# Seven block products for two thirds of the feed-forward pairs of a two-layer trunk

## The chip, the cores and the metric

The kernel runs on one core of a Trainium2 chip. The metric is the device time of one execution in microseconds, the median of several runs; lower is better. TensorE multiplies, VectorE and ScalarE do elementwise work, GpSimd a few sums, and SyncE issues most transfers. The trace records every instruction of one profiled execution.

## What is computed

The reference is a trunk of two layers on 512 tokens of width 1024, all in float32. Layer 0 mixes with a causal convolution module, layer 1 with differential attention. Each layer then has a SwiGLU feed-forward of width 2816 and a gated per-layer input. The change touches the feed-forward alone:

```python
def swiglu(x, w_gate, w_up, w_down):
    return (jax.nn.silu(x @ w_gate) * (x @ w_up)) @ w_down
...
for i in range(DEPTH):
    h = h + (conformer_conv(rms_norm(h, ...)) if i % 2 == 0 else diff_attention(rms_norm(h, ...)))
    u = rms_norm(h, ffn_norm_g[i])
    h = h + swiglu(u, ffn_w_gate[i], ffn_w_up[i], ffn_w_down[i])
    gate = jax.nn.sigmoid(rms_norm(h, ple_norm_g[i]) @ ple_w_gate[i])
    h = h + gate * (p[i] @ ple_w_proj[i])
```

## The kernel before

**Layout.** Activations lie transposed: features on the 128 partitions, the 512 tokens along the row. The residual is eight tiles `h[0..7]` of 128 x 512. A weight tile of 128 x 1024 holds one chunk of 128 output features, as eight blocks of 128 x 128, one for each chunk of the input features.

**Precision.** A float32 product is made of three float32r products. Each operand is split into a high part (a ScalarE copy to float32r) and a low part (the rest, by a VectorE subtraction). `mm3` (L153 to L157) multiplies low by high, high by low and high by high into one PSUM tile. `weight()` (L137 to L151) loads the next tile into `wraw` (two buffers, SyncE's queue), copies it into `whi` on ScalarE (L148) and subtracts into `wlo` on VectorE (L150); `whi` and `wlo` have four buffers each.

**Norms.** `Norm.chunk` (L179) scales a residual chunk by its gain, splits it into the tiles A0 to A15, and sums the squares. The factor 1/rms of each token, `rb`, comes later (`diagonal`, `rows`), so the feed-forward multiplies its products by `rb` afterwards (L582, L584).

**The feed-forward** (`ffn`, L566 to L596) goes through the 22 chunks of hidden features in three parts of 8, 8 and 6 (`PARTS`). For each chunk it loads a gate and an up tile, makes 24 matmuls of 512 columns for each into PSUM tiles `pg` and `pu`, multiplies by `rb`, applies Silu on ScalarE (L583), multiplies (L585) and splits the result into a hidden tile B (L587, L588). After a part, `linear` (L538) multiplies the part's hidden tiles by the down weights, one output chunk after another, the first two together, and `add` (L592) adds to the residual; in the last part each finished residual chunk goes on to the next norm.

**Names used below.** A chunk is one hidden chunk, a pair is two neighbouring ones. PSUM has the tags `mm` (four buffers), `sc` (two) and `tp` (two). In SBUF `wk` has four, `big` five buffers. `pp` is the projection of the per-layer input, made before and held in C and D tiles. The attention's `stage_s` (L755) puts the scores of a head's two halves into the two halves of one `sc` tile when they are at most 256 wide, and reads each on VectorE (L775 to L778). The last chunk of the last `ple` (L598) is made as two runs of 24 matmuls of 256 columns (`CUTS`).

**What sets the order.** The kernel is written in one order; a planner then fixes the order of each engine's own queue at build time, from its estimate of when each instruction is ready, and sets the waits and the reuse of buffers. On the chip each queue is worked in that fixed order.

Of the kernel before, what the change touches and what calls it, by code (L numbers as in the profile page):

```python
# [12 lines left out]
F32 = mybir.dt.float32  # L13
F32R = mybir.dt.float32r
AF = mybir.ActivationFunctionType
ALU = mybir.AluOpType
# [4 lines left out]
P = 128  # L21
S = 512
D = 1024
NC = D // P
# [52 lines left out]
PACK = True  # L77
E1 = True
GLO = 1
QKV = (("q", 0, (0, 0, 0, 0)), ("v", 0, (0, 1, 1, 0)), ("q", 1, (1, 1, 2, 2)), ("q", 2, (0, 1, 2, 0)), ("v", 1, (1, 2, 2, 2)), ("q", 3, (0, 2, 0, 1)))  # L80


@with_exitstack
def trunk(ctx, tc, xT, pT, wts, diag, dww, vec, rel, onehot, lamv, out):
    nc = tc.nc
    V, A, G, T = nc.vector, nc.scalar, nc.gpsimd, nc.tensor
# [19 lines left out]
    big = lambda dt=F32, shape=(P, S): sb(list(shape), "big", 5, dt)  # L106
    f = lambda ap: ap.bitcast(F32)
# [6 lines left out]
    def col(name, i=0):  # L114
        a, _ = VEC[name]
        return vt[:, a + i : a + i + 1]
# [7 lines left out]
    t = wk()[:, 0:P]  # L124
# [4 lines left out]
    t = tp()  # L129
# [4 lines left out]
    wnext = [0]  # L134
    loaded = [None]

    def weight(n=1024, pieces=1, between=(), eng=V, after=None):  # L137
        i = wnext[0]
        wnext[0] += 1
        raw = sb([P, 1024], "wraw", 2)  # L140
        hi = sb([P, 1024], "whi", 4, F32R)
        lo = sb([P, 1024], "wlo", 4, F32R)
        for k in range(pieces):
            cut = slice(k * n // pieces, (k + 1) * n // pieces)
            loaded[0] = nc.sync.dma_start(raw[:, cut], wts[i, :, cut])
            if k < len(between):
                between[k]()
            A.copy(hi[:, cut], raw[:, cut])  # L148
            with tc.issue_after(after.ins) if after else nullcontext():
                eng.tensor_tensor(lo[:, cut], raw[:, cut], f(hi[:, cut]), ALU.subtract)  # L150
        return hi, lo  # L151

    def mm3(acc, a, b, first, last):  # L153
        (ah, al), (bh, bl) = a, b
        T.matmul(acc, al, bh, start=first, stop=False)  # L155
        T.matmul(acc, ah, bl, start=False, stop=False)  # L156
        return T.matmul(acc, ah, bh, start=False, stop=last)  # L157
# [75 lines left out]
    norm = Norm("conv_g")  # L233
# [36 lines left out]
    y = []  # L270
# [160 lines left out]
    for c in range(NC):  # L431
        wa, wg = pairs[c]
        if c == 0:
            pg = half(wg)
            norm.diagonal()
            pa = half(wa)
            rb = norm.rows()
# [3 lines left out]
        if c > 0:  # L441
            pg = half(wg)
# [5 lines left out]
        tg, ta = big(), big()  # L448
# [59 lines left out]
    r = rsqrt_cols(vs[:, 0:4], 4, 1.0)  # L508
# [17 lines left out]
    z = []  # L526
# [36 lines left out]
    linear(NC, z, add_conv, 3, first=(None, last_add[0], scaled[1]))  # L563


    def ffn(norm, after):  # L566
        rb = None
        for at, (f0, n) in enumerate(PARTS):
            hid = []
            for i in range(n):  # L570
                wg, wu = weight(), weight()
                pg, pu = mm(), mm()
                for k in range(NC):
                    mm3(pg, wpart(wg, k), norm.u[k], k == 0, k == NC - 1)
                if rb is None:
                    norm.diagonal()
                for k in range(NC):
                    mm3(pu, wpart(wu, k), norm.u[k], k == 0, k == NC - 1)
                if rb is None:
                    rb = norm.rows()  # L580
                tg, tu = big(), big()
                V.tensor_tensor(tg, pg, rb, ALU.mult)  # L582
                A.activation(tg, tg, AF.Silu)  # L583
                V.tensor_tensor(tu, pu, rb, ALU.mult)  # L584
                V.tensor_tensor(tu, tu, tg, ALU.mult)  # L585
                hl = sb([P, 2, S], f"B{i}", 1, F32R)
                A.copy(hl[:, 0], tu)  # L587
                V.tensor_tensor(hl[:, 1], tu, f(hl[:, 0]), ALU.subtract)  # L588
                hid.append((hl[:, 0], hl[:, 1]))

            def add(m, acc):
                V.tensor_tensor(h[m], acc, h[m], ALU.add)  # L592
                if at == len(PARTS) - 1:
                    after.chunk(m)

            linear(n, hid, add, 2)  # L596
# [27 lines left out]
                gate(*part)  # L624

    n2 = Norm("ple_g0")
    ffn(norm, n2)
    norm = Norm("attn_g")
    ple(n2, pp, lambda m, cut: norm.chunk(m))

# [9 lines left out]
    for k in range(2):  # L640
        t = tp()
# [263 lines left out]
    norm = Norm("ffn_g1")  # L905
# [4 lines left out]

    linear(NC, ot, add_attn, 2, heads_until, step)
    n2 = Norm("ple_g1")
    ffn(norm, n2)

    def store(m, cut):
        nc.sync.dma_start(out[m][:, cut], h[m][:, cut])
# [30 lines left out]
def _layout(a):  # L947
# [25 lines left out]
    qkv = a["attn_w_qkv"][0]  # L973
    for what, at, _ in QKV:
        if what == "v":
# [70 lines left out]
```

## Time and profile before

| | us |
|---|---|
| median of 3 runs | 1307.87 (1307.86 to 1312.03) |
| the profiled execution: its span | 1308.0 |
| feed-forward of layer 0, part one: first products to first down sum | about 224 to 321 |
| part two: products, then down | 355 to 443, then to 487 |
| part three: products, then down | 487 to 553, then to 586 |
| feed-forward of layer 1, parts two and three | about 1030 to 1118 and 1162 to 1228 |

No separate device time is kept for the profiled execution; its span lies 0.1 us from the median. Times on the trace's rows count from the span's start. A row of the timeline has the start, the duration, the engine, the line, the operation, "out<-in" by the program's names with the shape, and in brackets the idle time before it with what ended it. A row of a grouped view has the count, the busy time, the mean duration in ns, and the idle time before the group's instructions. Two instructions of one engine can overlap by a little, so the distance between starts is what a full queue pays.

### The profile page before, as it was taken

To read this page: it belongs to the slowest core of one execution; us is meant where nothing else is said; L and a number is where in the kernel's file an instruction comes from. 1 tells how busy PE (TensorE), PEld (TensorE's weight loads), DVE (VectorE), ACT (ScalarE), POOL (GpSimd) and SP (SyncE) were. 2 spreads that over 40 slices of the span, in tenths; PEclk is the share of its full clock that TensorE was granted. 3 is DMA by queue.
4 is the path that set the end of the run, shared out by engine and by line. 5 is a ranking of instruction groups with operands and counts; after the bars stand their busy time and mean duration, and the time that the engine had idled before them with its cause. 6 is when DMAs were issued, how large, how long until landed. Compare 5 with 4: busy or idle time off the path is not lost. (4 is left out here: it accounts for less than half of the span.)

```text
span 1308.0 us, 15405 instructions
## 1 busy us (share of the span) xinstructions
PE 1278.6 (98%) x5904; PEld 1055.7 (81%) x5904; DVE 741.2 (57%) x1142; ACT 522.1 (40%) x827; POOL 248.2 (19%) x207
## 2 busy tenths in 40 slices
PE   8999999999999999999999998999999999999998
PEld 5888678888888888888888886878888888888887
DVE  6898646444344434456678888845543344334445
ACT  5642445332122212254566667734332233223332
POOL 4754323000000000032335535122000000000030
PEclk8999889999999999999999998999999999999999
DMA  6654313322323232232222211213323223222231
GB/s 219 229 166 156 106 33 129 96 98 87 106 96 97 88 104 94 80 122 83 80 91 92 89 58 59 87 48 114 97 97 97 97 97 97 97 97 89 83 119 65
DMA packets 46838, 131.97 MB, mean 101 GB/s; under 512 B 5379, under 2 KB 9987, under 8 KB 46764
## 3 DMA queue, kind: packets, MB, share of 16 engines
q1 hardware_dynamic: 44640, 127.55, 29.6%
q10 hardware_dynamic: 2124, 3.43, 0.8%
q8 instruction: 46, 0.75, 0.2%
q14 instruction: 28, 0.23, 0.1%
HBM read 126.75 MB, written 4.21 MB: 100 GB/s over the span
## 5 line engine op out<-in xcount | busy, mean ns | idle before, releaser
L148 ACT CAST whi<-wraw 128x1024 fp32r<-128x1024 f32 (+2 forms) x214 | 218.6, 1026 | 566.3 <-PE mm L157 349.5
L155 PE MATMUL mm<-A,wlo 128*128 128x512 f32 (+1 forms) x1096 | 423.9, 391 | 4.8 <-ACT A L169 2.7
L156 PE MATMUL mm<-A,whi 128*128 128x512 f32 (+1 forms) x1096 | 428.0, 392 | 0.4
L157 PE MATMUL mm<-A,whi 128*128 128x512 f32 (+1 forms) x1096 | 425.3, 389 | 0.0
L150 DVE TENSOR_TENSOR wlo<-wraw,whi 128x1024 fp32r<-128x1024 f32 (+2 forms) x210 | 260.5, 1244 | 70.9 <-ACT whi L148 70.6
L155 PEld LDWEIGHTS mm<-A,wlo 128*128 128x128 f32 x1096 | 206.2, 188 | 49.6 <-DVE wlo L150 3.7
L156 PEld LDWEIGHTS mm<-A,whi 128*128 128x128 f32 x1096 | 206.6, 188 | 46.4 <-DVE A L170 3.0
L157 PEld LDWEIGHTS mm<-A,whi 128*128 128x128 f32 x1096 | 206.6, 188 | 43.1 <-issue 1.0
L189 POOL TENSOR_TENSOR acc<-acc,wk 128x512 f32<-128x512 f32 x42 | 67.4, 1604 | 787.7 <-issue 660.2
L156 PE MATMUL mm<-B,whi 128*128 128x512 f32 x352 | 137.5, 391 | 0.0
L157 PE MATMUL mm<-B,whi 128*128 128x512 f32 x352 | 137.5, 391 | 0.0
L155 PE MATMUL mm<-B,wlo 128*128 128x512 f32 x352 | 137.2, 392 | 0.0
L592 DVE TENSOR_TENSOR h<-mm,h 128x512 f32<-128x512 f32 x48 | 33.0, 691 | 122.7 <-PE mm L157 122.7
L584 DVE TENSOR_TENSOR big<-mm,rb 128x512 f32<-128x512 f32 x44 | 30.4, 691 | 126.2 <-PE mm L157 126.2
L582 DVE TENSOR_TENSOR big<-mm,rb 128x512 f32<-128x512 f32 x44 | 30.4, 691 | 99.4 <-PE mm L157 93.0
L157 PEld LDWEIGHTS mm<-B,whi 128*128 128x128 f32 x352 | 66.1, 188 | 14.6
L155 PEld LDWEIGHTS mm<-B,wlo 128*128 128x128 f32 x352 | 66.1, 188 | 14.2
L156 PEld LDWEIGHTS mm<-B,whi 128*128 128x128 f32 x352 | 66.0, 188 | 14.2
L157 PE MATMUL mm<-whi,A 128*128 128x512 f32 x192 | 75.6, 395 | 0.0
L156 PE MATMUL mm<-wlo,A 128*128 128x512 f32 x192 | 75.0, 396 | 0.0
L155 PE MATMUL mm<-whi,A 128*128 128x512 f32 x192 | 74.8, 397 | 0.0
L214 POOL TENSOR_TENSOR r<-v,mhalf 128x8 f32<-128x8 f32 (+1 forms) x31 | 47.4, 1529 | 122.8 <-DVE v L212 100.4
(198 smaller groups left out, 1402.0 us busy)
## 6 DMA issues: line engine op xcount, KB each, us to landing
wraw<-in_wts SPq DMA_DIRECT2D x194, 512.0 KB, 3.5
wraw<-in_wts SPq DMA_DIRECT2D x16, 384.0 KB, 2.9
D<-in_diag SPq DMA_DIRECT2D x22, 256.0 KB, 4.9
C<-in_diag SPq DMA_DIRECT2D x16, 256.0 KB, 4.7
h<-in_xT SPq DMA_DIRECT2D x8, 256.0 KB, 5.6
bias<-scr ACTq DMA_DIRECT2D x8, 256.0 KB, 3.3
out_t<-h SPq DMA_DIRECT2D x7, 256.0 KB, 2.0
wraw<-in_wts SPq DMA_DIRECT2D x4, 256.0 KB, 5.2
```

The lines of the kernel that those rows point to most:

```text
L148: A.copy(hi[:, cut], raw[:, cut])
L150: eng.tensor_tensor(lo[:, cut], raw[:, cut], f(hi[:, cut]), ALU.subtract)
L155: T.matmul(acc, al, bh, start=first, stop=False)
L156: T.matmul(acc, ah, bl, start=False, stop=False)
L157: return T.matmul(acc, ah, bh, start=False, stop=last)
L189: self.last = self.eng.tensor_tensor(self.acc, self.acc, sq, ALU.add)
L214: last_pow[0] = G.tensor_tensor(r[:, :n], v[:, :n], mhalf[:, :n], ALU.pow)
L582: V.tensor_tensor(tg, pg, rb, ALU.mult)
L584: V.tensor_tensor(tu, pu, rb, ALU.mult)
L592: V.tensor_tensor(h[m], acc, h[m], ALU.add)
```

## The change

The first two pairs of a feed-forward stay as they are. While they run, a generator, stepped a few times in each chunk (`STEPS`), makes normed operands: `us[c]` = residual times gain times `rb`, split into `un[c]` in C and D tiles. From the third pair on the products use `un`, so nothing is multiplied by `rb` afterwards and Silu reads PSUM.

During the third and fourth pair the generator makes the combinations of the activations for seven block products: the operand is cut into four blocks, two halves of the input chunks (0 to 3 and 4 to 7) by two halves of the tokens (256 each). Four of the seven operands are differences of blocks, made by VectorE and split into the A tiles, which the raw operands have left by then; three are blocks themselves.

All pairs of parts two and three (four and three of them) then go through `strassen`, once for the two gate tiles and once for the two up tiles; one such run is called a group. `operands` makes the weight side: q gets the first halves of both weight tiles by a plain load, and an adding transfer on GpSimd's queue adds the second tile's two halves to them, so that two of the four weight sums come by transfer; the other two (s2, s4) are made by VectorE. Seven products of 4 blocks, 12 matmuls of 256 columns each, fill four PSUM tiles in the order 1, 5, 7, 2, 6, 4, 3, and VectorE combines them with seven sums (five instructions). A group takes four buffers each of `whi` and `wlo`.

```diff
-    def ffn(norm, after):
+    def ffn(norm, after, space):
...
+        def normed():
+            us = []
+            for c in range(NC):
...
+                V.scalar_tensor_tensor(t, h[c], col(norm.g, c), rb, ALU.mult, ALU.mult)
...
+                A.copy(hi, t)
+                V.tensor_tensor(lo, t, f(hi), ALU.subtract)
+                un.append((hi, lo))
+                yield
...
+            for c in (0, 2):
+                n3, t2 = (wk(F32, (P, 2, H2)) for _ in range(2))
+                for name in (5, 7, 6, 4):
...
+                    for j in range(2):
...
+                        V.tensor_tensor(t[:, j], x, y, ALU.subtract)
+                    i = 2 * (4 * (c // 2) + (5, 7, 6, 4).index(name))
+                    hi, lo = (sb([P, 2, H2], f"A{i + j}", 1, F32R) for j in range(2))
+                    A.copy(hi, t)
+                    V.tensor_tensor(lo, t, f(hi), ALU.subtract)
...
+        def operands(i):
+            turn[0] += 1
+            q = sb([P, 2, S], qtags[turn[0] % 3], 2)
+            nc.sync.dma_start(q, bass.AP(wts.tensor, wts.offset + i * P * 1024, [[1024, P], [2 * P * 1024, 2], [1, S]]))
+            nc.gpsimd.dma_start(q, wts[i + 2].rearrange("p (a s) -> p a s", a=2), accum_op=ALU.add)
+            r = sb([P, 2, S], "wraw", 2)
+            nc.sync.dma_start(r, wts[i].rearrange("p (a s) -> p a s", a=2))
+            z = sb([P, S], "bias", 2)
+            nc.sync.dma_start(z, wts[i + 2, :, S:])
...
+            p = ring()
+            split(flat(r), *p)
+            w[1], w[2] = half(p, first), half(p, low)
+            p = ring()
+            split(flat(q), *p)
+            w[7], w[5] = half(p, first), half(p, low)
+            s2, s4 = sb([P, S], "wth", 2), sb([P, S], "wtl", 2)
+            V.tensor_tensor(s2, q[:, 1], r[:, 0], ALU.add)
+            V.tensor_tensor(s4, s2, r[:, 1], ALU.add)
+            p = ring()
+            w[6], w[3] = half(p, first), half(p, low)
+            split(s2, *w[6])
+            split(s4, *w[3])
+            p = ring()
+            w[4] = half(p, first)
+            split(z, *w[4])
+            return w
+
+        def strassen(i):
+            w = operands(i)
+            def product(acc, name):
+                for k in range(4):
+                    mm3(acc, wpart(w[name], k), comb[name][k], k == 0, k == 3)
+            one, two, three, four = sc(), mm(), mm(), tp()
+            t, e, g = wk(), big(), big()
+            first, second = slice(0, H2), slice(H2, S)
+            product(one[:, first], 1)
+            A.copy(t[:, first], one[:, first])
+            A.mul(t[:, second], one[:, first], -1.0)
+            product(three[:, first], 5)
+            product(three[:, second], 7)
+            product(two[:, first], 2)
+            product(two[:, second], 6)
+            V.tensor_tensor(e, two, t, ALU.add)
+            V.tensor_tensor(
+                g.rearrange("p (a s) -> p a s", a=2), three.rearrange("p (a s) -> p a s", a=2),
+                e[:, second].unsqueeze(1).to_broadcast([P, 2, H2]), ALU.add,
+            )
+            V.tensor_tensor(e[:, second], three[:, second], g[:, first], ALU.add)
+            product(four[:, second], 4)
+            V.tensor_tensor(g[:, second], four[:, second], g[:, second], ALU.add)
+            product(four[:, first], 3)
+            V.tensor_tensor(g[:, first], four[:, first], g[:, first], ALU.subtract)
+            return e, g
...
+                if (at, pair) in SEVEN:
...
+                    gs = strassen(i)
+                    for t in gs:
+                        A.activation(t, t, AF.Silu)
+                    us = strassen(i + 1)
+                    for o, (t, g) in enumerate(zip(us, gs)):
+                        V.tensor_tensor(t, t, g, ALU.mult)
...
+                        A.copy(hs, t.rearrange("p (a s) -> p a s", a=2))
+                        V.tensor_tensor(ls, t.rearrange("p (a s) -> p a s", a=2), f(hs), ALU.subtract)
+                    continue
+                x = norm.u if seen < RAW_PAIRS else un
```

`RAW_PAIRS` is 2, `STEPS` is (0, 2, 3, 3) and two in every later chunk, `SEVEN` lists the pairs of parts two and three, and `SPACE` names the C and D tiles that each layer's feed-forward may use: with one of six buffers held by `pp`, three turn as q.

More of the change, by code (lines that the diff above doesn't have):

```diff
@@ L563, in trunk, with feed, ring, split @@
     linear(NC, z, add_conv, 3, first=(None, last_add[0], scaled[1]))
-    def ffn(norm, after):
+    def ffn(norm, after, space):
+        qtags, utags = space
         rb = None
+        un = []
+        comb = {}
+        uses = [None]
+        def normed():
+            us = []
+            for c in range(NC):
+                if c < 6:
+                    if c % 2 == 0:
+                        two = sb([P, 2, S], qtags[c // 2], 2)
+                    t = two[:, c % 2]
+                else:
+                    t = sb([P, S], "wth", 2)
+                us.append(t)
+                V.scalar_tensor_tensor(t, h[c], col(norm.g, c), rb, ALU.mult, ALU.mult)
+                tags = utags[c]
+                if len(tags) == 1:
+                    hi, lo = both(sb([P, 2, S], tags[0], 2, F32R))
+                else:
+                    hi, lo = (sb([P, S], t_, 1, F32R) for t_ in tags)
+                A.copy(hi, t)
+                V.tensor_tensor(lo, t, f(hi), ALU.subtract)
+                un.append((hi, lo))
+                yield
+            uses[0] = un
+            comb[1] = [tuple(t[:, :H2] for t in un[k]) for k in range(4)]
+            comb[2] = [tuple(t[:, :H2] for t in un[4 + k]) for k in range(4)]
+            comb[3] = [tuple(t[:, H2:] for t in un[4 + k]) for k in range(4)]
+            while uses[0] is not None:
+                yield
+            for k in (5, 7, 6, 4):
+                comb[k] = []
+            for c in (0, 2):
+                n3, t2 = (wk(F32, (P, 2, H2)) for _ in range(2))
+                for name in (5, 7, 6, 4):
+                    t = t2 if name == 6 else n3 if name == 7 else wk(F32, (P, 2, H2))
+                    for j in range(2):
+                        top, low = us[c + j], us[4 + c + j]
+                        b11, b12, b21, b22 = top[:, :H2], top[:, H2:], low[:, :H2], low[:, H2:]
+                        x, y = {5: (b12, b11), 7: (b12, b22), 6: (b11, n3[:, j]), 4: (b21, t2[:, j])}[name]
+                        V.tensor_tensor(t[:, j], x, y, ALU.subtract)
[3 more added lines that the diff above has]
+                    V.tensor_tensor(lo, t, f(hi), ALU.subtract)
+                    comb[name] += [(hi[:, j], lo[:, j]) for j in range(2)]
+                    yield
+        making = [normed()]
+        def feed(n=1):
+            for _ in range(n):
+                if making:
+                    try:
+                        next(making[0])
+                    except StopIteration:
+                        making.pop()
+        turn = [0]
+        def ring():
+            return [sb([P, 1024], t, 4, F32R) for t in ("whi", "wlo")]
+        def split(raw, hi, lo):
+            A.copy(hi, raw)
+            V.tensor_tensor(lo, raw, f(hi), ALU.subtract)
+        def operands(i):
[7 more added lines that the diff above has]
+            nc.sync.dma_start(z, wts[i + 2, :, S:])
+            first, low = slice(0, S), slice(S, 2 * S)
+            flat = lambda t: t.rearrange("p a s -> p (a s)")
+            half = lambda w, c: tuple(t[:, c] for t in w)
+            w = {}
+            p = ring()
[34 more added lines that the diff above has]
+                e[:, second].unsqueeze(1).to_broadcast([P, 2, H2]), ALU.add,
+            )
+            V.tensor_tensor(e[:, second], three[:, second], g[:, first], ALU.add)
[4 more added lines that the diff above has]
+            return e, g
+        seen = 0
@@ L568, in ffn @@
         for at, (f0, n) in enumerate(PARTS):
             hid = []
[L570 to L589, printed above, removed]
+            for pair in range(n // 2):
+                hi, lo = (sb([P, 2, S], f"B{2 * pair + k}", 1, F32R) for k in range(2))
+                for k in range(2):
+                    hid.append((hi[:, k], lo[:, k]))
+                if (at, pair) in SEVEN:
+                    i = wnext[0]
+                    wnext[0] += 4
+                    gs = strassen(i)
[4 more added lines that the diff above has]
+                        V.tensor_tensor(t, t, g, ALU.mult)
+                        first, step = (H2, H2) if o else (0, S + H2)
+                        hs, ls = (bass.AP(x.tensor, x.offset + first, [list(x.ap[0]), [step, 2], [1, H2]]) for x in (hi, lo))
+                        A.copy(hs, t.rearrange("p (a s) -> p a s", a=2))
+                        V.tensor_tensor(ls, t.rearrange("p (a s) -> p a s", a=2), f(hs), ALU.subtract)
+                    continue
+                x = norm.u if seen < RAW_PAIRS else un
+                for i in range(2):
+                    wg, wu = weight(), weight()
+                    pg, pu = mm(), mm()
+                    for k in range(NC):
+                        mm3(pg, wpart(wg, k), x[k], k == 0, k == NC - 1)
+                    if rb is None:
+                        norm.diagonal()
+                    for k in range(NC):
+                        mm3(pu, wpart(wu, k), x[k], k == 0, k == NC - 1)
+                    if rb is None:
+                        rb = norm.rows()
+                    tg, tu = big(), big()
+                    if x is un:
+                        A.activation(tg, pg, AF.Silu)
+                        V.tensor_tensor(tu, pu, tg, ALU.mult)
+                    else:
+                        V.tensor_tensor(tg, pg, rb, ALU.mult)
+                        A.activation(tg, tg, AF.Silu)
+                        V.tensor_tensor(tu, pu, rb, ALU.mult)
+                        V.tensor_tensor(tu, tu, tg, ALU.mult)
+                    A.copy(hi[:, i], tu)
+                    V.tensor_tensor(lo[:, i], tu, f(hi[:, i]), ALU.subtract)
+                    feed(STEPS[2 * seen + i] if 2 * seen + i < len(STEPS) else 2)
+                seen += 1
+                if seen == RAW_PAIRS:
+                    assert len(un) == NC, len(un)
+                    feed()
+                    uses[0] = None
@@ L626, in trunk @@
     n2 = Norm("ple_g0")
-    ffn(norm, n2)
+    ffn(norm, n2, SPACE[0])
     norm = Norm("attn_g")
@@ L912, in trunk @@
     n2 = Norm("ple_g1")
-    ffn(norm, n2)
+    ffn(norm, n2, SPACE[1])
     def store(m, cut):
```

7 lines of the change are left out of this document (added).

## The prediction

> **What bounds the kernel now.** First the page's totals:
>
> ```profile
> span 1308.0 us, 15405 instructions
> PE 1278.6 (98%) x5904; PEld 1055.7 (81%) x5904; DVE 741.2 (57%) x1142; ACT 522.1 (40%) x827; POOL 248.2 (19%) x207
> ```
>
> TensorE is busy nearly all the time; VectorE has 43% to spare on average. An average hides stages, so next the busy times by stage: the first feed-forward's part one (224 to 312), two (355 to 443) and three (487 to 553), and, for later use, four stages in which VectorE is loaded harder.
>
> ```profile
> 33.00:65.00 32.00, 31.69 (x176) 26.97 (x175) 28.84 (x34) 19.17 (x28) 22.79 (x17) 1.00 0.66 226
> 65.00:98.00 33.00, 31.17 (x174) 26.86 (x173) 29.68 (x36) 16.07 (x23) 16.85 (x14) 1.00 0.51 167
> 224.00:312.00 88.00, 88.00 (x392) 72.65 (x391) 42.87 (x53) 26.95 (x34) 3.20 (x2) 1.00 0.29 96
> 355.00:443.00 88.00, 88.00 (x389) 72.84 (x389) 39.93 (x48) 26.07 (x32) 0.00 (x0) 1.00 0.29 96
> 487.00:553.00 66.00, 66.00 (x293) 54.64 (x292) 29.20 (x36) 18.63 (x24) 0.00 (x0) 1.00 0.28 86
> 700.00:760.00 60.00, 58.39 (x303) 49.27 (x302) 52.58 (x130) 42.54 (x96) 34.94 (x35) 1.00 0.24 79
> 760.00:820.00 60.00, 53.27 (x278) 45.11 (x277) 49.72 (x141) 41.72 (x99) 25.30 (x26) 0.91 0.23 74
> ```
>
> The columns are stage, length, busy PE, PEld, DVE, ACT, POOL with counts, granted clock, DMA share, GB/s. In the feed-forwards PE is busy without a gap, at clock 1.00, with VectorE at 40 to 49%. The list of waits for parts two and three says the same:
>
> ```profile
> DVE big L584 <- PE mm L157: 44.3, 14, 3.6
> ```
>
> VectorE waits for matmuls there, 14 times for 3.2 us. The stage is matmul time, so fewer matmul columns shorten it, as long as VectorE and the queues keep up.
>
> **TensorE's part.** In part two the same VectorE instruction, released by the same matmul, comes seven chunks apart at:
>
> ```profile
> 360.01 0.69 DVE L582 TENSOR_TENSOR big<-mm,rb 128x512 f32<-128x512 f32 x1 [3.15 <-PE mm L157]
> ...
> 436.17 0.69 DVE L582 TENSOR_TENSOR big<-mm,rb 128x512 f32<-128x512 f32 x1 [2.21 <-PE mm L157]
> ```
>
> 76.16/7 = 10.88 us a chunk of 48 matmuls, 226.7 ns for each of 512 columns; a pair of chunks is 96 matmuls, 21.76 us. The change turns a pair into 2 groups (gate, up) x 7 products x 4 blocks x 3 = 168 matmuls of 256 columns. That width stands at the end of the kernel, 48 in a row:
>
> ```profile
> 1297.69 0.28 PE L155 MATMUL mm<-A,wlo 128*128 128x256 f32 x1
> ...
> 1303.32 0.28 PE L157 MATMUL mm<-A,whi 128*128 128x256 f32 x1
> ```
>
> 5.63/47 = 119.8 ns, more than half of 226.7: about 13 ns a matmul do not shrink. So a pair costs 168 x 0.1198 = 20.13 us and saves 1.63, not an eighth of 21.76 (2.72). Seven pairs in each of two feed-forwards: 14 x 1.63 = 22.9 us off, 1285.1 if nothing else waits. The Trainium skill (TensorE: Matmul & The Clock Gate, Back-to-back issue gap) gives N/2.4 + 2.5 ns for a warm isolated matmul, 215.8 and 109.2 ns; by it the gain would be 33.2 us and the time 1274.8 (estimate). This trace has 11 ns more on each matmul, which counts double at half the width, so the rows decide.
>
> **VectorE's part.** Its prices, back to back and in a dependent chain:
>
> ```profile
> 529.17 0.69 DVE L584 TENSOR_TENSOR big<-mm,rb 128x512 f32<-128x512 f32 x1 [3.08 <-PE mm L157]
> 529.97 0.69 DVE L585 TENSOR_TENSOR big<-big,big 128x512 f32<-128x512 f32 x1
> 530.58 1.22 DVE L150 TENSOR_TENSOR wlo<-wraw,whi 128x1024 fp32r<-128x1024 f32 x1
> 531.72 0.68 DVE L588 TENSOR_TENSOR B<-big,B 128x512 fp32r<-128x512 f32 x1
> ...
> 1301.67 0.42 DVE L612 TENSOR_TENSOR big<-big,C 128x256 f32<-128x256 f32 x1 [0.48 <-ACT big L611]
> 1302.13 0.42 DVE L613 TENSOR_TENSOR h<-h,big 128x256 f32<-128x256 f32 x1
> ```
>
> Start to start an independent 512 takes 0.61, a 1024 1.14; a 512 that needs the one before 0.80, a 256 that does 0.46. The 1024's and 512's starts run 0.08 under their durations, so an independent 256 is taken at 0.34 (estimate).
> A group now has: two 1024 splits, 2.28; sums s2 and s4 and three 512 splits, 5 x 0.61, with 0.19 because s4 needs s2, 3.24; the sums after the products, e 0.61, g 0.80, e's second half 0.46, two 256s 0.68, together 2.55. That is 8.07; a pair has two, and two times a product and a split, 4 x 0.61 = 2.44: 18.58 us of the pair's 20.13, 92%. Before it was 4 x 1.14 + 8 x 0.61 = 9.44 of 21.76. VectorE stays under TensorE, by 1.55 us a pair, but its queue is in order: each of the sums waits for a product, with the next group's operand splits queued behind it, and for those TensorE waits.
> What such a load costs TensorE is bounded by stages of this kernel. At best nothing (part two). In 33 to 98 VectorE is 58.52/65 = 90% busy and PE idle 65 - 62.86 = 2.14 us, 3.3%; in 700 to 820 VectorE is 85% busy beside shorter instructions and PE idle 8.34 of 120, 7%. Of 14 x 20.13 = 282 us that is 0, 9.3 or 20 us. I take 9.3: the first stage too cuts weights ahead of dense matmuls. The sum: 1308.0 - 22.9 + 9.3 = 1294.4.
>
> **ScalarE** has longer copies:
>
> ```profile
> L148 ACT CAST whi<-wraw 128x1024 fp32r<-128x1024 f32 x17 | 17.9, 1053 | 63.4 <-PE mm L157 32.2 <-issue 31.2
> L583 ACT ACTIVATE big<-big 128x512 f32<-128x512 f32 x8 | 5.0, 626 | 0.0
> ```
>
> A group has two of 1.05, three of 0.63 and two of 256, at most 0.63: 5.25; with two Silus and two copies 13.0 a pair, 65%. It hides.
>
> **Part one.** The normed operands add 8 scalings and 8 splits, and the combinations 8 x (two 256 differences and a 512 split). A scaling is half of this row:
>
> ```profile
> 897.85 1.40 DVE L170 SCALAR_TENSOR_TENSOR A<-h,vec,A 128x512 fp32r<-128x512 f32 x2
> ```
>
> 8 x (0.70 + 0.61) + 8 x (0.68 + 0.61) = 20.8 us, less 8 x 0.61 for the multiplications by rb that the third and fourth pair lose. VectorE was 42.87 of 88 busy and has 45 free, so I price this at nothing; without that cover the third pair would wait for its operands, up to 8 x 1.31 = 10.5 us a feed-forward. The down products are unchanged; at the ends of parts two and three their first 36 and 24 matmuls, 8.2 and 5.4 us, do not need the last pair, whose last sums, copies and splits take under 3.
>
> **The loads.** For a group SyncE issues a plain load into q, then r and half a tile z; GpSimd adds 512 KB onto q once the plain load has landed.
>
> ```profile
> wraw<-in_wts SPq DMA_DIRECT2D x194, 512.0 KB, 3.5
> L189 POOL TENSOR_TENSOR acc<-acc,wk 128x512 f32<-128x512 f32 x42 | 67.4, 1604 | 787.7 <-issue 660.2
> ```
>
> No trace here shows an adding transfer. From below it is the plain 3.5 us, from above twice that (it also reads its target) and a GpSimd instruction of 1.6: 8.6. With the load before it 7 to 12 us. q has three buffers, so the load can go out when group n-3 is done with its own, some two groups (20 us) ahead. Behind a q that waits for its buffer stand r and z on SyncE's queue, which have a group's slack; behind the adding transfer on GpSimd stands nothing until the norm's sums in part three's down products (POOL 0.00 in 355 to 443). DMA traffic goes from 0.29 to about 0.29 x 1.75 x 21.76/20.13 = 0.55. I take nothing.
>
> **Rivals.** *Slower: one bank, two readers' turns.* Products 4 and 3 go to two halves of one PSUM tile, and VectorE reads the first half between them. The attention's packed scores show what becomes of such a tile:
>
> ```profile
> 831.99 0.22 PE L775 MATMUL sc<-C,C 128*128 128x128 f32 x1
> ...
> 832.16 0.33 PE L775 MATMUL sc<-C,C 128*128 128x256 f32 x1
> ...
> 832.36 0.29 DVE L778 CUSTOM_DVE_ANT_0 big<-sc,bias 128x128 f32<-128x128 f32 x1
> ...
> 834.40 0.28 PE L775 MATMUL sc<-C,C 128*128 128x128 f32 x1
> ```
>
> The second half's matmul (834.40) comes only behind the first half's read (832.36), as the Trainium skill asks (PSUM — Partial Sum Buffer, PSUM bank collisions raise a hardware error: even disjoint columns of a bank must be guarded); the trace agrees. So product 3 waits for the chain e, g, e, g after product 6: 0.80 + 0.80 + 0.46 + 0.42 = 2.48 us, of which product 4 covers 12 x 0.1198 = 1.44. That leaves 1.0 us, 2.2 with a 1.14 us split in front, times 28 groups: 29 to 61 us, so 1314 to 1346. It decides from 22.9/28 = 0.82 us a group on. Against it: in the same rows the next tile's matmul (832.16) was put in between, so the next group's product 1 (1.44 us) can fill this wait; its weights' buffer is free after product 2, 2.9 us before, and needs a copy 1.05 and a split 1.22. Chance 0.15.
> *VectorE becomes the bound.* If it loses 2.4 to 3.8 us a pair waiting, a pair takes 21.0 to 22.4: 1297 to 1317, middle 1307. For: by durations, as the stages' shares are counted, a group is 2 x 1.22 + 7 x 0.69 + 3 x 0.42 = 8.53 and a pair 19.8, 98%, more than any stage above. Against: TensorE then waits too, which gives VectorE its inputs. Chance 0.14.
> *The adding transfer is late.* If load and addition take 15 us a group and do not overlap, 28 x 5 = 140 us: 1425 and more. Chance 0.05.
> *Weight loads bind.* One took 192 ns beside the 256-wide matmuls:
>
> ```profile
> L157 PEld LDWEIGHTS mm<-A,whi 128*128 128x128 f32 x16 | 3.1, 192 | 0.0
> ```
>
> End to end, 168 x 0.192 = 32.3 a pair: 1455. But at 119.8 ns a matmul they already overlap. Chance 0.01.
>
> **The numbers.** The span, 1308.0, is within 0.2 us of the median, 1307.87, and nothing is added around it. Forecast 1294, chance 0.65, its own range 1285 to 1305. The range 1284 to 1324 reaches over VectorE's case and a third of the bank's; 0.10 is left above there, 0.06 with the two last rivals, and 0.04 below. 0.3% (3.9 us) is what a measurement can tell. Faster: 0.64 of the forecast and 0.04 of VectorE's case, 0.68. Same: 0.01 and 0.06, 0.07. Slower: 0.15 + 0.04 + 0.05 + 0.01 = 0.25.
>
> **What would show it.** Right: 256-wide matmuls about 120 ns apart, pairs of 20.1 to 21.6 us, VectorE near 90% in parts two and three, product 1 of the next group ahead of product 3. Wrong: PE idle before one product in every group, released by VectorE (the bank); PE idle before first products, released by wlo splits (VectorE); VectorE idle on a DMA into q.

## The result and the profile after

The changed kernel takes 1289.18 us (median of 4 runs, 1288.43 to 1292.58); before takes 1307.93 beside it (4 runs, 1307.86 to 1312.03). The ratio is 0.986, with a 95% interval of 0.984 to 0.9879: 18.8 us faster, where 1294 was forecast. The profiled execution of the changed kernel took 1288.43 us at a span of 1286.3, so 2.1 us lie around the span; the two profiled spans differ by 21.7 us.

The page's totals and the loads' rows of the changed kernel (KB each, median us from issue to landing):

```profile
span 1286.3 us, 18032 instructions
...
PE 1253.5 (97%) x6912; PEld 1082.9 (84%) x6912; DVE 886.0 (69%) x1430; ACT 603.9 (47%) x999; POOL 268.4 (21%) x235
...
C<-in_wts SPq DMA_DIRECT2D x28, 512.0 KB, 4.5
C<-in_wts POOLq DMA_DIRECT2D x28, 512.0 KB, 6.0
```

TensorE is still the busy engine. Its instructions went from 5904 to 6912 and its busy time fell by 25 us; VectorE took 145 us more. The average again says little, so here are the stages: busy time by engine in the first feed-forward's part one, in the products of parts two and three, and in one pair (columns as in the prediction).

```profile
224.00:312.00 88.00, 88.00 (x392) 72.60 (x392) 56.45 (x83) 34.90 (x49) 4.84 (x5) 1.00 0.46 133
352.20:432.60 80.40, 79.68 (x661) 79.22 (x660) 63.00 (x97) 42.56 (x68) 6.13 (x7) 1.00 0.63 162
478.20:537.30 59.10, 59.10 (x493) 58.98 (x492) 45.19 (x69) 30.87 (x50) 1.74 (x2) 1.00 0.37 101
370.88:391.04 20.16, 20.16 (x171) 20.16 (x170) 17.81 (x29) 11.05 (x18) 1.74 (x2) 1.00 0.68 178
```

A pair takes 20.16 us with TensorE busy throughout (20.13 predicted), VectorE 17.81 (18.58 predicted), ScalarE 11.05 (13.0). In the eight groups of part two TensorE stands idle for 0.72 of 80.40 us. One pair is not the whole part: over part two VectorE is busy for 63.00 of 80.40 us (78%), over part three for 45.19 of 59.10 (76%), since a part's first operands and last sums lie beside the down products.

**Where the time went.** The first row of part two, of part three and of what follows, in the timeline of before and then of the changed kernel; each stretch holds the part's products and its down products:

```profile
354.35 0.39 PE L155 MATMUL mm<-A,wlo 128*128 128x512 f32 x1
...
485.43 0.39 PE L155 MATMUL mm<-A,wlo 128*128 128x512 f32 x1
...
583.37 0.39 PE L155 MATMUL mm<-A,wlo 128*128 128x512 f32 x1
```

```profile
352.16 0.28 PE L163 MATMUL sc<-C,wlo 128*128 128x256 f32 x1
...
478.18 0.28 PE L163 MATMUL sc<-C,wlo 128*128 128x256 f32 x1
...
571.50 0.39 PE L163 MATMUL mm<-A,wlo 128*128 128x512 f32 x1
```

| layer 0 | before | after | shorter by | by 1.63 us a pair |
|---|---|---|---|---|
| part two and its down products | 131.08 | 126.02 | 5.06 | 6.52 |
| part three and its down products | 97.94 | 93.32 | 4.62 | 4.89 |

In layer 1 the same rows (1028.73, 1159.81, 1257.75 before; 1017.50, 1142.35, 1235.69 after) give 6.23 and 4.60. Together 20.5 us, of 22.9 by the matmuls' price; so 2.4 us are lost, where the prediction had put 9.3. The remaining 1.2 us of the spans' difference lie outside (2.2 us ahead of the feed-forward, 1.0 given back behind it): before enters the first feed-forward's norm sums at 230.08 and the changed kernel at 227.89. That front stage was not edited, and in the profiles of the runs below these sums stand anywhere from 226.2 to 232.4, so it is spread between executions.

**Why the bank wait is not seen.** The timeline of the changed kernel around one group's products 4 and 3 (tiles `tp`), from which the rows of the steps are taken:

```profile
379.51 0.28 PE L163 MATMUL tp<-A,wlo 128*128 128x256 f32 x1
...
380.95 0.28 PE L163 MATMUL sc<-C,wlo 128*128 128x256 f32 x1
...
384.80 0.41 DVE L702 TENSOR_TENSOR big<-tp,big 128x256 f32<-128x256 f32 x1
...
387.92 0.28 PE L163 MATMUL tp<-C,wlo 128*128 128x256 f32 x1
...
389.56 0.42 DVE L704 TENSOR_TENSOR big<-tp,big 128x256 f32<-128x256 f32 x1 [0.34 <-PE tp L165]
389.60 0.28 PE L163 MATMUL tp<-A,wlo 128*128 128x256 f32 x1
...
391.04 0.28 PE L163 MATMUL sc<-C,wlo 128*128 128x256 f32 x1
```

Product 4 starts at 379.51 and VectorE reads it (L702) at 384.80, far behind the products. But product 3 of that group stands at 387.92 in TensorE's queue: products 1, 5, 7, 2 and most of 6 of the next group, 381 to 388, were put between. The planner moved it back by nearly five products, where the prediction had thought of one; in the 28 groups it is three to five, 4.3 to 7.3 us. So VectorE's turn at the bank has other matmuls over it. No matmul is listed as waiting for that read, and one weight load, at 408.61:

```profile
PEld tp L163 <- DVE big L702: 0.2, 1, 0.2
```

**The one gap.** TensorE's 0.72 us in part two, followed back in the same timeline, and the list of waits for 352 to 433 with the rows on TensorE's and VectorE's inputs (us in all, times, longest):

```profile
398.37 1.21 DVE L643 TENSOR_TENSOR wlo<-wraw,whi 128x1024 fp32r<-128x1024 f32 x1
...
399.61 0.33 SPq L652 DMA_DIRECT2D wraw<-in_wts  x1
...
401.35 0.38 SPq L649 DMA_DIRECT2D C<-in_wts  x1
...
407.20 0.69 DVE L666 TENSOR_TENSOR wth<-C,wraw 128x512 f32<-128x512 f32 x1 [2.88 <-DMA wraw<-in_wts]
...
412.54 1.21 DVE L643 TENSOR_TENSOR wlo<-C,whi 128x1024 fp32r<-128x1024 f32 x1
...
413.90 0.36 PE L163 MATMUL mm<-A,wlo 128*128 128x256 f32 x1 [0.72 <-DVE wlo L643]
```

```profile
DVE wth L666 <- DMA wraw<-in_wts: 3.5, 2, 2.9
...
PE mm L163 <- DVE wlo L643: 0.7, 1, 0.7
```

SyncE issues r's load at 399.61, when the split from 398.37 has freed one of r's two buffers. The sum s2 is next in VectorE's queue, so VectorE waits for that load until 407.20, 2.88 us; then it works with hardly a pause up to the split of q (412.54), and that is the split for which TensorE stands. So "r and z have a group's slack" did not hold here: the load took 7.5 us to land, twice the median of such loads in this kernel (3.7). The adding transfer (issued at 397.73) and the load into the next q (401.35) were under way beside it, and the DMA engines were 84% busy from 399.6 to 407.2; whether that is what made it late was not tested. The same pause made VectorE's read of product 4 late (408.14), for which the weight load at 408.61 waited.

### The profile page after: what moved, and what is told of

Its sections match the earlier page's. It is cut to its first block, busy times and chain, and to the rows that moved or that the text cites. A ratio compares the mean times of both kernels' runs of the same rounds, so it can differ in the third digit from the quotient of the medians.

```text
span 1286.3 us, 18032 instructions
## 1 busy us (share of the span) xinstructions
PE 1253.5 (97%) x6912; PEld 1082.9 (84%) x6912; DVE 886.0 (69%) x1430; ACT 603.9 (47%) x999; POOL 268.4 (21%) x235
## 5 line engine op out<-in xcount | busy, mean ns | idle before, releaser
L163 PE MATMUL mm<-A,wlo 128*128 128x512 f32 (+1 forms) x856 | 295.2, 350 | 5.6 <-ACT A L177 2.6
L164 PE MATMUL mm<-A,whi 128*128 128x512 f32 (+1 forms) x856 | 298.6, 350 | 0.3
L165 PE MATMUL mm<-A,whi 128*128 128x512 f32 (+1 forms) x856 | 296.5, 347 | 0.0
L156 ACT CAST whi<-wraw 128x1024 fp32r<-128x1024 f32 (+2 forms) x158 | 159.5, 1016 | 253.6 <-PE mm L165 120.0
L158 DVE TENSOR_TENSOR wlo<-wraw,whi 128x1024 fp32r<-128x1024 f32 (+2 forms) x154 | 196.3, 1278 | 86.3 <-ACT whi L156 86.1
L163 PEld LDWEIGHTS mm<-A,wlo 128*128 128x128 f32 x856 | 162.8, 190 | 28.5 <-DVE wlo L158 3.9
L164 PEld LDWEIGHTS mm<-A,whi 128*128 128x128 f32 x856 | 162.9, 190 | 24.2 <-DVE A L178 3.5
L165 PEld LDWEIGHTS mm<-A,whi 128*128 128x128 f32 x856 | 162.8, 190 | 20.6 <-issue 1.0
L650 POOL DMA_DIRECT2D C<-in_wts x28 | 24.6, 878 | 520.0 <-DVE h L759 228.9
L163 PE MATMUL mm<-C,wlo 128*128 128x512 f32 (+1 forms) x212 | 74.1, 350 | 0.0
L164 PE MATMUL mm<-C,whi 128*128 128x512 f32 (+1 forms) x212 | 73.8, 348 | 0.0
```

The source lines that it names most:

```text
L650: nc.gpsimd.dma_start(q, wts[i + 2].rearrange("p (a s) -> p a s", a=2), accum_op=ALU.add)
```

## The experiments

The theory to test: the gain comes from TensorE alone (14 pairs with 168 matmuls of 119.8 ns in place of 96 of 226.7 ns), VectorE's extra work and the adding transfer are hidden, and the bank would have cost time but for the order of the products. Ratios are to before, run on the same chip (medians 1308.72, 1310.17 and 1307.73 in the three sets).

### The price of a matmul of 256 columns

Before's feed-forward, parts two and three, with each run of 24 matmuls cut into two runs of 256 columns: the same columns, twice the instructions.

```diff
-                for k in range(NC):
-                    mm3(pg, wpart(wg, k), norm.u[k], k == 0, k == NC - 1)
+                cuts = [slice(0, S)] if at == 0 else [slice(0, S // 2), slice(S // 2, S)]
+                for cut in cuts:
+                    for k in range(NC):
+                        mm3(pg[:, cut], wpart(wg, k), tuple(t[:, cut] for t in norm.u[k]), k == 0, k == NC - 1)
...
```

The up tile's products (`pu`) are cut in the same way.

> The kernel before, with the gate and up products of parts two and three made as two runs of 24 matmuls of 256 columns in place of one of 24 with 512; nothing else changes. Theory (about 13 ns of each matmul do not shrink with its width): 192 x 0.1198 = 23.0 us a pair against 21.76, 14 x 1.24 = 17 us slower, 1322 to 1328. Rival (the 119.8 ns at the end of the kernel were special to that place, a narrow matmul costs half of a wide one): 1308, within 3 us.

1327.18 us, ratio 1.0155 (1.014 to 1.017): 18.5 us slower. The groups by shape in 360 to 440:

```profile
L156 PE MATMUL mm<-A,whi 128*128 128x256 f32 x223 | 63.1, 283 | 0.0
```

Three such groups of 223, one for each of mm3's lines, fill the 80 us without idle time: 80/669 = 119.6 ns each. So half the width costs 53% of the time, and the 13 ns that do not shrink are real. An eighth fewer columns would have been worth 2.72 us a pair; the part of each matmul that does not shrink takes 1.1 of it back.

### The normed operands without the products

```diff
-SEVEN = ((1,0),(1,1),(1,2),(1,3),(2,0),(2,1),(2,2))
+SEVEN = ()
```

> The changed kernel with an empty list of seven-product pairs: normed operands from the third pair on and the combinations are still made, but all pairs use 96 matmuls of 512 columns. Theory (the gain is the saved matmul columns): as the kernel before, 1306 to 1310. Rival (part of the gain comes from the normed operands, which take the multiplications by rb off VectorE): below 1304.

1307.82 us, ratio 0.9997 (0.9988 to 1.0007). Its feed-forwards, from the first matmul of the norm's sums to the first of the next norm's, take 361.46 and 361.45 us, as before's (361.45 both). The normed operands and the activations' combinations cost nothing and gain nothing: the whole gain is the products'.

### The bank, with the product's place forced

In the first kernel every product of a group is held behind product 3 of the group before, so that TensorE's order is the one written and product 3 comes right behind product 4. The second kernel does the same and gives product 3 the free half of product 1's tile instead of product 4's.

```diff
+        third = [None]
...
+            before = third[0]
+
             def product(acc, name):
-                for k in range(4):
-                    mm3(acc, wpart(w[name], k), comb[name][k], k == 0, k == 3)
+                with tc.issue_after(before.ins) if before else nullcontext():
+                    for k in range(4):
+                        end = mm3(acc, wpart(w[name], k), comb[name][k], k == 0, k == 3)
+                if name == 3:
+                    third[0] = end
```

```diff
-            product(four[:, first], 3)
-            V.tensor_tensor(g[:, first], four[:, first], g[:, first], ALU.subtract)
+            product(one[:, second], 3)
+            V.tensor_tensor(g[:, first], one[:, second], g[:, first], ALU.subtract)
```

> The changed kernel with every product of a group held behind product 3 of the group before in TensorE's queue, so that product 3 stands right behind product 4. Theory (the two halves of one bank make product 3 wait for VectorE's read, and the planner had hidden that by moving other products in between): TensorE idle 1.0 to 2.2 us before each product 3, released by VectorE, 29 to 61 us over 28 groups, 1318 to 1350. Rival (the read is early enough, the wait is small anyway): under 0.3 us a group, 1289 to 1297.

> As the run before (product 3 held right behind product 4), but product 3 goes to the free second half of product 1's tile, another bank, so that no read of product 4's half stands before it. Theory (the shared bank is the cost): the wait before product 3 is gone, 1288 to 1296. Rival (the fixed order costs, because next products may not run ahead while operands are late): as slow as the run before, within 5 us.

The first: 1376.9 us, ratio 1.0536 (1.0512 to 1.0559). The second: 1287.35, 0.985 (0.9835 to 0.9865), just under the range expected. So the order as written costs nothing, and the shared bank, where nothing is put in between, costs 89.5 us, 3.2 a group. That it costs was expected; the 1.0 to 2.2 a group was too little. TensorE's waits in the first kernel, and the timeline of one group, show why (this kernel's lines are numbered six higher than the changed kernel's):

```profile
PE tp L163 <- DVE big L708: 50.8, 24, 2.2
```

```profile
378.81 0.68 DVE L701 TENSOR_TENSOR big<-mm,wk 128x512 f32<-128x512 f32 x1
378.90 0.28 PE L163 MATMUL tp<-A,wlo 128*128 128x256 f32 x1
379.52 0.69 DVE L702 TENSOR_TENSOR big<-mm,big 128x512 f32<-128x512 f32 x1
380.73 0.42 DVE L706 TENSOR_TENSOR big<-mm,big 128x256 f32<-128x256 f32 x1
381.06 0.41 DVE L708 TENSOR_TENSOR big<-tp,big 128x256 f32<-128x256 f32 x1
...
381.53 0.39 PE L163 MATMUL tp<-C,wlo 128*128 128x256 f32 x1 [2.11 <-DVE big L708]
...
386.00 0.28 PE L163 MATMUL mm<-A,wlo 128*128 128x256 f32 x1
```

The chain e, g, e, g of the prediction is there row by row, and product 3 waits 2.11 us for its end, near the upper bound. Such waits add up to 50.8 us, not to 89.5. But the 24 matmuls from 381.53 to 386.00 then take 4.47 us instead of 2.88. Its busy times by stage give the reason:

```profile
352.00:440.00 88.00, 75.25 (x536) 73.16 (x535) 56.07 (x86) 34.41 (x56) 5.27 (x6) 0.90 0.52 126
...
381.50:386.00 4.50, 4.47 (x24) 4.47 (x25) 4.26 (x8) 1.26 (x3) 0.87 (x1) 0.62 0.32 88
```

The granted clock, 1.00 in all the feed-forward stages shown of both kernels, is 0.90 here and 0.62 right after the wait. A wait of 2.1 us and 1.6 us of slow matmuls behind it make 3.7 us in this group; 3.2 is the mean of all 28. The Trainium skill (TensorE: Matmul & The Clock Gate, HAM oscillation — how this bites in real kernels) warns of idle gaps above about 3.4 us; in this run gaps of 2.1 us, one in each 14 us, went with the lower clock.

Then product 3 in its own bank, with the order left to the planner:

> The changed kernel, its queue order left to the planner, with product 3 in the second half of product 1's tile, so that it shares no bank with product 4. Theory (the planner already hid the bank wait, 2.4 us of waits are left in all): 1285 to 1290. Rival (moving product 3 behind the next group's products still costs, because its late sum holds up the next split): under 1285.

1289.5 us, 0.9853 (0.9826 to 0.9881). Beside the changed kernel (0.986) that is no difference in the time. But the planner's order is another one here: behind product 4 (from 363.62 in its timeline) stand two products on `sc` tiles, from 365.06, and ScalarE copies the next group's product 1 only at 368.20, behind both. So product 3 stands right behind product 4, as in the second kernel above, and no run has the own bank with the moved order. What the run shows is that the changed kernel's way, shared bank and moved products together, costs next to nothing. (The last set below measures it more finely.)

### How much room VectorE has

The sum s2 is made three or five times, which adds 2.44 or 4.88 us of VectorE work a pair and changes no value.

```diff
-            V.tensor_tensor(s2, q[:, 1], r[:, 0], ALU.add)
+            for _ in range(5):
+                V.tensor_tensor(s2, q[:, 1], r[:, 0], ALU.add)
```

> The changed kernel with the sum s2 made three times over in each group, two more VectorE instructions of 0.61 us, 2.44 us a pair, with the same result. Theory (VectorE is busy 17.8 of a pair's 20.1 us in the trace, so 2.3 us are free): 20.25 of 20.13, at the edge, 0 to 6 us slower than the changed kernel, 1288 to 1295. Rival (VectorE's queue already sets the pace through its order): all of it shows, 14 x 2.44 = 34 us, about 1323.

> The same with four more VectorE instructions in each group, 4.88 us a pair. Theory (VectorE becomes the bound past 2.3 us a pair): 17.8 + 4.9 = 22.7 a pair against 20.1, 14 x 2.6 = 36 us slower than the changed kernel, 1318 to 1332, slower than the kernel before. Rival (its queue already sets the pace): 14 x 4.88 = 68 us, about 1357. Third (there is more room than the busy time says): under 1305.

With three: 1288.52 us, 0.9849 (0.9818 to 0.9881), no slower than the changed kernel. With five: 1295.43, 0.9902 (0.987 to 0.9934), far under the 1318 to 1332 that the sum per pair had given; the third expectation came true. Busy times around part two of the changed kernel, and of the kernel with five (last products of part one and down products; products of part two; down products), then part two of the kernel with three:

```profile
320.00:352.00 32.00, 32.00 (x141) 26.17 (x140) 15.52 (x19) 6.01 (x7) 0.87 (x1) 1.00 0.39 111
352.00:432.00 80.00, 79.28 (x657) 78.77 (x656) 62.40 (x96) 42.49 (x68) 6.13 (x7) 1.00 0.63 162
432.00:478.00 46.00, 46.00 (x212) 38.04 (x211) 24.75 (x33) 10.66 (x13) 0.87 (x1) 1.00 0.46 131
```

```profile
320.00:354.00 34.00, 34.00 (x150) 27.80 (x149) 23.32 (x31) 7.36 (x8) 0.87 (x1) 1.00 0.35 97
354.00:434.00 80.00, 78.46 (x646) 77.63 (x645) 73.18 (x117) 40.60 (x66) 6.14 (x7) 1.00 0.62 163
434.00:480.00 46.00, 46.00 (x217) 38.34 (x217) 29.90 (x43) 12.17 (x14) 0.00 (x0) 1.00 0.44 127
```

```profile
354.00:434.00 80.00, 80.00 (x657) 79.26 (x656) 68.28 (x106) 40.90 (x66) 6.14 (x7) 1.00 0.65 165
```

With five, VectorE's time among the products rose by only 10.8 us; by 7.8 it rose before them and by 5.2 behind, beside down products, which leave VectorE about half free. The comparison of a pair's 20.13 us with its own VectorE work holds for pairs inside a part. A part is short, four pairs, and its first operands and its last sums lie outside it. So VectorE was 91% busy in 354 to 434 and TensorE lost 1.5 of the 80 us. From the second group to the fifth the starts lie 10.08 us apart, then 10.87, 11.09 and 10.48: the limit is there, but late in the part. With three, VectorE is 85% busy over part two and TensorE has no gap there at all.

### Without the adding transfer

The second weight tile is loaded whole, into the two raw buffers that r uses, and VectorE makes the sum that the transfer made.

```diff
+WR = 2
...
-            nc.gpsimd.dma_start(q, wts[i + 2].rearrange("p (a s) -> p a s", a=2), accum_op=ALU.add)
-            r = sb([P, 2, S], "wraw", 2)
+            x = sb([P, 2, S], "wraw", WR)
+            nc.sync.dma_start(x, wts[i + 2].rearrange("p (a s) -> p a s", a=2))
+            V.tensor_tensor(q, q, x, ALU.add)
+            r = sb([P, 2, S], "wraw", WR)
...
-            z = sb([P, S], "bias", 2)
-            nc.sync.dma_start(z, wts[i + 2, :, S:])
+            z = x[:, 1]
```

> The changed kernel without the adding transfer: the second tile is loaded whole beside the first (both in the two raw buffers) and VectorE adds it onto q, one more instruction of 1.14 us a group, 2.28 us a pair. Theory (VectorE has 2.3 us a pair free): 0 to 6 us slower than the changed kernel, 1288 to 1295; should the two raw buffers hold up the loads, VectorE and ScalarE idle on transfers and it is more. Rival (the adding transfer is late in some groups and costs time itself): faster than the changed kernel, under 1287.

1344.29 us, 1.0263 (1.0229 to 1.0298). VectorE's time is not what decides, as the busy times of part two show, and TensorE's and ScalarE's waits in the whole of this kernel:

```profile
352.00:440.00 88.00, 77.41 (x606) 75.76 (x605) 67.89 (x103) 39.28 (x65) 0.00 (x0) 0.96 0.41 121
```

```profile
PE sc L164 <- DVE wlo L644: 34.9, 18, 3.2
```

```profile
ACT whi L643 <- DMA wraw<-in_wts: 79.7, 26, 6.8
```

VectorE is 77% busy, under the 91% that the run above carried. ScalarE's copies wait 79.7 us for loads into the raw buffers, two of which now serve twice the tiles, and TensorE waits 34.9 us for splits, which come behind such copies, again at a lower clock (0.96 in part two). So in this kernel the transfer's worth is at least that it needs no further raw buffer. Whether VectorE could make the sums at no cost with more of them is open; it was not tried.

### More of the same, and both together

All on one chip: the changed kernel again; the own bank with the order held, again; the fourth pair of part one by seven products too; and that with own bank and order held.

```diff
-STEPS = (0, 2, 3, 3)
-SEVEN = ((1,0),(1,1),(1,2),(1,3),(2,0),(2,1),(2,2))
+STEPS = (0, 2, 3, 3, 4, 4)
+SEVEN = ((0,3),(1,0),(1,1),(1,2),(1,3),(2,0),(2,1),(2,2))
```

> The changed kernel once more, beside the three others of this call on the same chip: 0.985 to 0.987 of the kernel before, 1287 to 1291.

> The version with product 3 in its own bank and in fixed order once more. Theory (its products run without a gap, 2.4 us of waits in the changed kernel are gone): 1 to 3 us under the changed kernel. Rival (the difference lay between two calls): within 1 us of it.

> The changed kernel with one more pair as seven products, the fourth of part one, in each feed-forward: all eight combinations are then made during the third pair, four a chunk. Theory (each pair saves 1.63 us while operands are early): 2 x 1.63 = 3.3 us under the changed kernel, 1285 to 1287. Rival (its first weights sums cannot be loaded before the combinations free the buffers that q uses, some 10 us of load and adding transfer, so TensorE waits): 0 to 15 us over the changed kernel.

> The same additional pair on the version with product 3 in its own bank and in fixed order. Theory: 3.3 us under that version, 1283 to 1285. Rival (late q): 0 to 15 us over it.

| | us | ratio to before | feed-forward, layer 0 / 1 |
|---|---|---|---|
| before | 1307.73 | 1 | 361.45 / 361.45 |
| changed kernel | 1291.67 | 0.9874 (0.9855 to 0.9892) | 350.85 / 351.11 |
| own bank, order held | 1287.11 | 0.9836 (0.9816 to 0.9857) | 350.25 / 350.25 |
| one more pair | 1286.12 | 0.9821 (0.9803 to 0.9839) | 349.04 / 349.04 |
| one more pair, own bank, order held | 1283.26 | 0.9809 (0.979 to 0.9829) | 348.67 / 348.67 |

The last column is the distance from the first matmul of the feed-forward's norm sums to the first of the next norm's, in the profiled execution; it leaves the front stage's spread out. By 22.9/2 = 11.45 us off each it should be 350.0 where nothing waits. With the own bank and the order held it is 350.25, in both layers: the matmuls' sum is the floor, to 0.25 us. In the run with the own bank and the order left to the planner it is 350.25 in both layers too. The changed kernel loses 0.6 and 0.9 us more here, 1.5 and 0.4 in its first profile. Whether the shared bank or the moved products cost that is open, since no run parts the two. What the traces show is VectorE's wait for r (s2, "DVE wth" on "DMA wraw"): 3.5 us over part two in layer 0 of the changed kernel and 2.0 in this second profile of it, 0.2 or 0.3 with the own bank, where TensorE has no gap in these parts. The extra pair gives 1.6 us with the order held (350.25 to 348.67), as 1.63 says. The times' medians differ by more than these distances (4.6 us for the own bank, where the distances say 1.5), and their intervals touch, so the distances are the better measure. The changed kernel came out just above the 1287 to 1291 expected of it, and the own bank's 4.6 us under it is more than the 1 to 3 expected; its distances stay inside. The two runs with the extra pair came where they were expected. The last version is 24.5 us under before, faster than both kernels.

## Why the prediction was right

**TensorE's part was right to two percent.** 22.9 us at 119.8 ns; `narrow` gives the same price by itself, the pair takes 20.16 us against 20.13, and a feed-forward without waits takes 350.25 against 350.0, so the matmuls alone gave 22.4 (2 x 11.2). By the Trainium skill's isolated gap (TensorE: Matmul & The Clock Gate, Back-to-back issue gap) the gain would have been 33.2 (estimate); the runs decide for the rows of the trace.

**The mis-sized term is "What such a load costs TensorE": 9.3 us, and the runs show 2.4.** The price came from another stage with a load of 90% on VectorE and TensorE 3.3% idle, set against the 92% worked out for a pair. That load holds inside a pair (88%), but not over a part: 78% and 76% in parts two and three. And the load alone does not set the loss: in the kernel with three sums VectorE was 85% busy over part two and TensorE never idle, in the changed kernel 78%, and TensorE idle for 0.72 us. The loss in layer 0's part two is 1.5 us. Of it the one gap is followed, 0.72 us, where VectorE had stood still for a load with the splits for TensorE behind it; the rest of it, and the 0.3 us that each of the other three parts lost, is not. Why such waits were rare is argued, not shown. The sums stand well behind their products (L702 reads product 4 3.9 us after its end), but with the own bank they stand nearer (1.8 us in `banks`, 365.06 to 366.87) and less is lost. The lower end of the bounds, nothing, was close. The run with 4.88 us more a pair, 91% busy over part two, has feed-forwards of 353.51 and 353.73 us, 7.2 us over twice 350.0, and so comes near the value that I took for this load.

**"Nothing is added around it" was wrong by 1.8.** In every later run of before 1.7 to 1.9 us lie around the span, so its profiled execution took about 1309.8 (estimate: 1308.0 + 1.8), 1.9 us above its median; that is most of why the two profiled spans differ by 21.7 us and the medians by 18.8. The sum made from it, 1309.8 - 22.9 + 2.4 = 1289.3, is 0.9 us above the changed kernel's profiled execution (1288.43): 1.2 us were saved outside the feed-forwards, less 0.3 that lies around its span beyond before's 1.8.

**The hidden parts were hidden.** Part one: TensorE 88.00 of 88, VectorE 56.45 against 42.87, 13.6 us more against 15.9 worked out; `seven_off` puts its cost at nothing. The adding transfer landed within its bounds of 3.5 to 8.6, but for a tail of half a microsecond; the view of its line (duration of GpSimd's instruction in ns, shortest, median and longest, then the landing):

```profile
L650 POOL DMA_DIRECT2D C<-in_wts x28: 853/872/1053, 263.4 to 1166.9; - x28
...
DMA to landing us min/median/max: 5.2/6.0/9.1
```

The plain load (4.5) and it (6.0) together took 10.5 us, inside 7 to 12, and the list of waits for part two has none of VectorE or ScalarE for q. The DMA share was priced at 0.55 and came to 0.63 in part two, 0.68 in the pair; the late load of r is the one place where that may have counted.

**The rivals.** The bank is a true mechanism: forced, it costs 3.2 us a group, from 1287 to 1377. It did not come because three to five products, not one, were put in between; the reason given against it was right in kind. The rows of the attention's scores had shown only an order (the second half's matmul at 834.40 starts 1.75 us after the read from 832.36 has ended); that it is a wait, and its price, came from `forced`. VectorE as the bound shows only beyond 2.44 us more a pair. The late transfer and the weight loads (192 ns each, overlapped at 119.6 ns a matmul) did not come.

## What to carry to other kernels

Price a narrower matmul by a row of the same width, not by its columns: here half the width costs 53%. When a busy engine gets more work, ask which of its instructions waits, and what another engine needs from behind it in the queue; the share of busy time in one pair gave four times the loss that came, and a part of four pairs was less loaded than one pair inside it. And look where the build puts a dependent step in the queue before paying for its wait: the same two products in one bank cost next to nothing with three to five others between them and 3.2 us side by side.

## What the runs showed of the hardware

TensorE's granted clock fell with waits shorter than 3 us: in `forced`, 2.1 us of idle time once in 14 us left 0.62 for the 4.5 us after it and 0.90 in the mean of part two, and in the group shown such a wait cost another 1.6 us (24 matmuls in 4.47 us in place of 2.88). The single gap of 0.72 us in the changed kernel left the clock at 1.00. Weight loads of 0.19 us each ran beside matmuls that start 0.12 us apart, with TensorE busy throughout. An adding transfer of 512 KB took 6.0 us where the plain load beside it took 4.5, and 0.88 us of GpSimd to issue.
